# Two changes to the norms of a two-layer encoder: where the squares are summed, and who adds the old x

## The chip, the cores and the metric

The kernel runs on one core of a Trainium2 chip. A core has five engines that run side by side, each through its own list of instructions in order: TensorE (PE, matmuls), VectorE (DVE), ScalarE (ACT), GpSimd (POOL), and SyncE (SP), which here only issues DMAs. They meet by semaphores: an instruction that needs another engine's result waits, and everything behind it on its engine waits too. The metric is the device time of one execution in microseconds (us); lower is better. Before the change it is 2510.55 us, the median of 3 runs (2510.04 to 2511.96).

## The reference

Two layers are applied, with the same weights, to two groups of 512 and 256 tokens of 1024 channels. Cut to what matters here:

```
def _rmsnorm(x, gain):
    xf = xf * lax.rsqrt(jnp.mean(xf * xf, axis=-1, keepdims=True) + EPS)
    return xf * gain

for l in range(2):
    h = _rmsnorm(x, norm_mix_pre[l])          # the norm that begins a layer
    mix = ... projections, four attentions, gates, w_out of h ...
    x = x + _rmsnorm(mix, norm_mix_post[l])   # middle of a layer
    hf = _rmsnorm(x, norm_ffn_pre[l])
    f = _conv_ffn(hf, ...)
    x = x + _rmsnorm(f, norm_ffn_post[l])     # end of a layer
```

Between the two layers there are thus two norms in a row: `x + _rmsnorm(f, norm_ffn_post[0])`, and at once `_rmsnorm` of that sum with `norm_mix_pre[1]`, whose result h feeds the first matmuls of the second layer.

## The kernel before, in words

**Layout.** Activations lie transposed, with channels on the 128 partitions: x is 8 blocks of 128 channels by 768 tokens (512 + 256), kept in DRAM between norms. The tokens are cut into three groups of 256, G0, G1 and G2, so that the norms of one group can run while PE works on another. Every operand of a matmul is split into a high and a low part in float32r, and each product is three matmuls (high by high, high by low, low by high), L842 to L854.

**A norm.** `pre_norm` (L716) makes h for one group. ACT squares four tiles of 128x512 (two channel blocks by 256 tokens each). A sum over channels is a sum over partitions, which PE does by matmuls against a column of 1/1024: `mean_square` gives four small matmuls for one such tile (`b<-const,p`, 128x2; each is two passes in the trace, so x8). Then `rstd_bcast`: DVE adds epsilon (L499), POOL takes the power -0.5 (L505), PE transposes that value over all partitions (L464). Then DVE multiplies the four tiles, ACT copies the high part of h, and DVE subtracts to make the low part. The gain is multiplied in place beforehand, on ACT. With `easy` (the norm in the middle of a layer) the four squares are summed on DVE first and PE sums one tile; without it (the first norm of the kernel, and the norm between the layers) each tile has its own mean square on PE.

**Between the layers.** `grouped_tail` ends the down projection group by group. When a group is through, `sandwich` (L786) runs for it: loads the old x into four buffers `p` by DMA, takes the mean square of the group (already collected in `msq`), multiplies by 1/rms, adds the old x, stores the new x (`x<-g`), and calls `pre_norm` for the next layer. While it does, PE goes on with the tail of the next group, and after G2's tail with the first matmuls of the next layer, which take h of G0, then G1, then G2 (`v_tiles` and `job_V`: per group 96 matmuls of 256 columns).

**The order.** `Flow` is a planner that runs while the program is built: it keeps a clock per engine with a cost for each operation, and whoever is ready first gets its instructions written next. So a changed cost or dependence moves instructions on all engines near it. On the chip each engine then follows its list. There are 12 buffers `p`, 13 `g` (the residual tiles `g` of this norm among them), 4 PSUM buffers `b` and 2 `d`.

**Names.** `p` squares and loads, `g` the residual tiles, `b` and `d` PSUM, `st` the rstd values, `h` the normed input, `raw` and `w` a weight unit before and after its split, `x` in DRAM. L460 is every matmul, L464 every transpose, L476 every ACT operation, L490 every tensor_tensor on DVE, L509 every DMA.

Of the kernel before, what the change touches and what calls it, by code (L numbers as in the profile page):

```python
# [20 lines left out]
ALU = mybir.AluOpType  # L21
# [411 lines left out]
class Trunk:  # L433
# [74 lines left out]
    def dma(self, out, in_, *deps):  # L508
# [3 lines left out]
            nbytes *= s  # L512
        return self.f.on("dma", max(nbytes / 340.0, 450), *deps) + 2000


    def w_init(self):
        self.w_fetched = self.w_split = self.w_used = 0
        self.w_raw, self.w_ready = {}, {}
        self.w_allowed = 0
        self.spare = True  # L520
        self.parts = []
        self.tail_keys = {("out", m) for m in range(KB - TAIL_OUT, KB)}
        self.tail_keys |= {("down", len(CHUNKS) - 1, m) for m in range(KB - TAIL_DOWN, KB)}
        self.w_total = self.depth * len(self.keys)
        self.steps = unit_steps(self.keys, self.depth)
        self.paired = {n + i for s, n in self.steps if s == "first" for i in range(2)}
# [191 lines left out]
    def pre_norm(self, G, x, gain, h, last, first=False, easy=False):  # L718


        c = slice(GRP * G, GRP * G + GRP)
        b = yield from self.B.get([128, 512], F32)
        for i, (ap, t, free) in enumerate(x):
            q = yield from self.P.get([128, 2, GRP], F32)
            if first:
                yield t
            t = q.t = self.act(q.ap, ap, AF.Square, t, q.t)
            if not easy:
                yield t
                t = self.mean_square(b, q.ap, not i, i == len(x) - 1, t)  # L730
                q.drop(t)
            elif i:
                t = sq.t = self.tt(sq.ap, sq.ap, q.ap, ALU.add, t, sq.t)
                q.drop(t)
            else:
                sq = q
        if easy:
            yield t
            t = self.mean_square(b, sq.ap, True, True, t)
            sq.drop(t)  # L740
        yield t
        r = self.rstd_bcast(b, 2, t)
        tn = next(r)
        xg = []
        for i, (ap, t, free) in enumerate(x):
            for j in range(2):
                t = self.copy(ap[:, j], ap[:, j], free, scale=gain[:, 2 * i + j : 2 * i + j + 1])
            xg.append(t)
        if first:
            self.w_allowed = max(self.w_allowed, 1)  # L750
            self.pump()
        yield tn
        for w in r:
            yield w
        for i, (ap, _, _) in enumerate(x):
            if easy:
                yield from self.calm()
            xg[i] = t = self.tt(ap, ap, self.over(b, 2), ALU.mult, xg[i], b.t)
        b.drop(t)
        for i, (ap, _, _) in enumerate(x):  # L760
            k = slice(2 * i, 2 * i + 2)
            t = self.copy(h[:, 0, k, c], ap, xg[i], h.t)
            if easy:
                yield from self.calm()
            t = self.tt(h[:, 1, k, c], ap, h.f32()[:, 0, k, c], ALU.subtract, t)
        last(t)
        self.h_ready[G] = t
        self.w_allowed = len(self.steps)
# [14 lines left out]
    def sandwich(self, G, mix, msq, x_old, x_new, pre, h, done=None):  # L783

        c = slice(GRP * G, GRP * G + GRP)
        easy = done is not None
        xs = []
        for i in range(4):  # L790
            x = yield from self.P.get([128, 2, GRP], F32)
            x.t = self.dma(x.ap, x_old[:, 2 * i : 2 * i + 2, c], x.t)
            xs.append(x)
        b = yield from self.B.get([128, 512], F32)
        sq = msq[G]
        self.add_square(sq)
        yield sq.t
        t = self.mean_square(b, sq.ap, True, True, sq.t)
        sq.drop(t)
        yield t  # L800
        yield from self.rstd_bcast(b, 2, t)
        new = []
        for i, m in enumerate(mix):
            if easy:
                yield from self.calm()
            t = self.tt(m[:, :, c], m[:, :, c], self.over(b, 2), ALU.mult, b.t, m.t)
            if easy:
                yield from self.calm()
            t = self.tt(m[:, :, c], m[:, :, c], xs[i].ap, ALU.add, xs[i].t, t)
            xs[i].drop(t)  # L810
            new.append((m[:, :, c], t, self.dma(x_new[:, 2 * i : 2 * i + 2, c], m[:, :, c], t)))
        b.drop(t)
        if h is None:
            for m in mix:
                m.drop(t + 2500)
        else:
            yield from self.pre_norm(G, new, pre, h, done or (lambda t: [m.drop(t) for m in mix]),
                                     easy=easy)
# [33 lines left out]
    def grouped_tail(self, tail, nk, key, rhs, wait, mix, msq, gain, sandwich, acc=None):  # L852


        m0 = KB - tail
        for m in range(m0):
            yield from self.mix_buf(mix, m)
            w = yield from self.weight(key(m))
            blk = yield from self.dblock()
            blk.t = yield from self.mblock(self.whole(blk), w, rhs, nk, wait=None if m else wait)  # L860
            w.drop()
            yield from self.mix_evac(blk.cols, blk, m, range(3), mix, msq, gain, acc)
        ws = []
        for G in range(3):
            for m in range(m0, KB):
                yield from self.mix_buf(mix, m)
                if G == 0:
                    w = yield from self.weight(key(m))
                    ws.append(w)
                w = ws[m - m0]  # L870
                blk = yield from self.bank(G == 2)
                c0 = GRP * G
                src = blk[:, 0:GRP]
                blk.t = yield from self.mblock([(src, c0, c0 + GRP)], w, rhs, nk)
                if G == 2:
                    w.drop()
                yield from self.mix_evac(lambda c0, c1: src, blk, m, [G], mix, msq, gain, acc)
            self.f.start(sandwich(G), 0)
# [843 lines left out]
    def g_wait(self, gs, f):  # L1722
        while len(gs[f]) < 2:
            yield self.f.now + 200
        while max(t for _, t in gs[f]) > self.f.now:
            yield max(t for _, t in gs[f])

    def ffn(self, gain, sandwich, box):
        gs = [[] for _ in range(NF)]
        self.up_over, self.a_dram, self.v_dram, self.gelus = False, {}, {}, {}  # L1730
# [288 lines left out]
```

## Time and profile before

| | |
|---|---|
| median of 3 runs | 2510.55 us |
| the profiled execution | 2509.54 us |
| its span, first to last instruction | 2507.7 us |
| PE busy | 2462.9 us, 98% |
| DVE busy | 1714.1 us, 68% |
| ACT busy | 1284.6 us, 51% |
| POOL busy | 41.3 us, 2% |
| mean granted clock of PE | 0.993 |

The span is cut at three places by what PE does. From 0 to 70.2 us it starts up: weights and x arrive, the first norm runs, and the first matmuls of layer 0 follow. From 1225.9 to 1312.0 us lies the border of the two layers. From 2450 us the last norm runs out. Elsewhere PE has hardly a gap. DVE, ACT and the DMAs matter only where PE waits for them.

### The profile page before, as it was taken

The page shows a single profiled execution, that of the slowest core. Times are in us where ns is not written, and L with a number is a line of the kernel's source. Part 1 is how long each engine was busy: PE and PEld are TensorE (multiplying, and loading weights), DVE is VectorE, ACT ScalarE, POOL GpSimd, SP SyncE. Part 2 cuts the span into 40 slices and gives each one's busy share as a digit, 9 for nine tenths or more (in the row PEclk, how much of TensorE's full clock was granted, in tenths as well). Part 3 has the DMA queues.
Part 4 walks back from the last instruction along what each step waited for, and adds up shares of the span by engine and source line. Part 5 has one row for each costly group of instructions (what it writes and reads, how often), then busy time and mean ns, then how long its engine had stood idle before and what let it go on. Part 6 is the DMA issues. An engine that isn't in the chain of part 4 may idle for free. (4 is left out here: it accounts for less than half of the span.)

```text
span 2507.7 us, 40638 instructions
## 1 busy us (share of the span) xinstructions
PE 2462.9 (98%) x15606; PEld 2295.4 (92%) x15606; DVE 1714.1 (68%) x3282; ACT 1284.6 (51%) x2496; POOL 41.3 (2%) x38
## 2 busy tenths in 40 slices
PE   7999999999999999999989999999999999999998
PEld 7998888888999999988988988888889999999887
DVE  3567666756468888786755676667564689887866
ACT  5565665532355655563545556655324555556533
POOL 0001000000000000000000010000000000000000
PEclk9999999999999999999989999999999999999999
DMA  3433355343333333363423432553433233333643
GB/s 116 136 113 97 104 159 147 111 135 120 102 118 118 112 110 108 112 219 122 142 74 130 126 102 79 168 144 122 141 104 127 90 117 114 121 118 120 201 141 105
DMA packets 163986, 309.93 MB, mean 124 GB/s; under 512 B 25936, under 2 KB 89808, under 8 KB 163792
## 3 DMA queue, kind: packets, MB, share of 16 engines
q1 hardware_dynamic: 163792, 307.34, 39.0%
q8 instruction: 123, 2.02, 0.3%
q14 instruction: 71, 0.58, 0.1%
HBM read 225.74 MB, written 62.65 MB: 115 GB/s over the span
## 5 line engine op out<-in xcount | busy, mean ns | idle before, releaser
L460 PE MATMUL d<-h,w 128*128 128x256 f32 (+2 forms) x5040 | 920.0, 332 | 0.0
L460 PEld LDWEIGHTS d<-h,w 128*128 128x128 f32 x5040 | 762.2, 189 | 79.1
L460 PE MATMUL d<-g,w 128*128 128x256 f32 (+2 forms) x2763 | 489.7, 332 | 4.1 <-ACT g L476 3.6
L460 PEld LDWEIGHTS d<-g,w 128*128 128x128 f32 x2763 | 436.7, 188 | 39.7 <-ACT g L476 7.6
L490 DVE TENSOR_TENSOR w<-raw,w 128x1024 fp32r<-128x1024 f32 (+3 forms) x216 | 237.9, 1104 | 188.5 <-ACT w L476 184.4
L476 ACT ACTIVATE w<-raw 128x1024 fp32r<-128x1024 f32 (+3 forms) x216 | 206.5, 958 | 106.1 <-PE d L460 69.9
L476 ACT ACTIVATE p<-p,st 128x512 f32<-128x512 f32 (+2 forms) x288 | 174.4, 612 | 159.8 <-DVE st L1185 82.3
L460 PE MATMUL b<-h,w 128*128 128x384 f32 (+2 forms) x1344 | 233.5, 328 | 0.0
L460 PEld LDWEIGHTS b<-h,w 128*128 128x128 f32 x1344 | 213.4, 189 | 9.8
L460 PE MATMUL b<-g,w 128*128 128x384 f32 (+2 forms) x1257 | 215.2, 324 | 0.0
L476 ACT ACTIVATE g<-d 128x384 f32<-128x384 f32 (+6 forms) x210 | 113.1, 546 | 198.5 <-PE d L460 174.5
L460 PEld LDWEIGHTS b<-g,w 128*128 128x128 f32 x1257 | 203.2, 188 | 2.9
L494 DVE SCALAR_TENSOR_TENSOR p<-g,par,p 128x511 f32<-128x511 f32 (+1 forms) x232 | 142.3, 615 | 12.4 <-ACT p L476 8.2
L490 DVE TENSOR_TENSOR g<-g,b 128x512 f32<-128x512 f32 (+2 forms) x180 | 105.7, 598 | 62.3 <-PE b L460 43.7
L476 ACT ACTIVATE p<-b 128x512 fp32r<-128x512 f32 (+3 forms) x182 | 96.1, 538 | 93.0 <-PE b L464 73.3
L490 DVE TENSOR_TENSOR p<-b,p 128x512 fp32r<-128x512 f32 (+1 forms) x164 | 101.0, 627 | 50.5 <-ACT p L476 42.8
L490 DVE TENSOR_TENSOR g<-g,d 128x768 f32<-128x768 f32 (+2 forms) x118 | 80.0, 681 | 74.3 <-PE d L460 74.2
L460 PE MATMUL b<-g,g 128*128 128x384 f32 (+2 forms) x384 | 106.7, 348 | 5.1 <-DVE st L1158 3.3
L476 ACT ACTIVATE p<-g,par 128x512 f32<-128x512 f32 (+1 forms) x116 | 81.5, 703 | 54.6 <-DVE g L490 53.8
L476 ACT ACTIVATE g<-p 128x512 fp32r<-128x512 f32 (+1 forms) x118 | 67.5, 574 | 79.7 <-DVE p L490 58.2
L460 PE MATMUL b<-p,g 128*128 128x256 f32 x576 | 94.9, 286 | 3.1 <-DVE p L490 3.1
L1158 DVE CUSTOM_DVE_ANT_0 p<-b,bi 128x512 f32<-128x512 f32 (+2 forms) x144 | 81.5, 566 | 22.9 <-PE b L460 19.3
(120 smaller groups left out, 3156.6 us busy)
## 6 DMA issues: line engine op xcount, KB each, us to landing
raw<-weights SPq DMA_DIRECT2D x206, 512.0 KB, 3.9
bi<-weights SPq DMA_DIRECT2D x48, 512.0 KB, 3.8
g<-g SPq DMA_DIRECT2D x128, 96.0 KB, 2.2
p<-v SPq DMA_DIRECT2D x44, 256.0 KB, 3.7
x<-g SPq DMA_DIRECT2D x36, 256.0 KB, 2.1
p<-x SPq DMA_DIRECT2D x36, 256.0 KB, 4.5
v<-g SPq DMA_DIRECT2D x18, 384.0 KB, 3.8
v<-p SPq DMA_DIRECT2D x26, 256.0 KB, 2.0
```

The source lines that it names most:

```text
L460: self.nc.tensor.matmul(out=out, lhsT=lhsT, rhs=rhs, start=start, stop=stop, skip_group_check=more)
L476: self.nc.scalar.activation(out=out, in_=in_, func=func, **k)
L490: self.nc.vector.tensor_tensor(out=out, in0=a, in1=b, op=op)
L494: self.nc.vector.scalar_tensor_tensor(out=out, in0=a, scalar=s, in1=b, op0=op0, op1=op1)
L1158: nc.vector.tensor_tensor_reduce(out=p[:, :nkey], in0=s[:, :nkey], in1=bt, scale=1.0, scalar=init, op0=ALU.add, op1=ALU.max, accum_out=mx[ ...
```

## The change

The first part is in `pre_norm`: without `easy` the squares are now summed on DVE as well (three adds of 128x512 per group), and PE takes the mean square of one tile where it took four. That holds for the three groups of the first norm and the three between the layers. The second part is in `sandwich`, between the layers only: the four loads of the old x and the four adds on DVE go; instead, after each multiplication, a DMA issued by POOL adds the old x from DRAM onto the tile in place. The stores of the new x are issued after that, one by one.

```
+    def dma_add(self, out, in_, *deps):
+        self.nc.gpsimd.dma_start(out=out, in_=in_, accum_op=ALU.add)
+        nbytes = 4
+        for s in out.shape:
+            nbytes *= s
+        return self.f.on("dma", max(nbytes / 170.0, 450), *deps) + 2500
...
             t = q.t = self.act(q.ap, ap, AF.Square, t, q.t)
-            if not easy:
-                yield t
-                t = self.mean_square(b, q.ap, not i, i == len(x) - 1, t)
-                q.drop(t)
-            elif i:
+            if i:
+                if first:
+                    yield t
                 t = sq.t = self.tt(sq.ap, sq.ap, q.ap, ALU.add, t, sq.t)
                 q.drop(t)
             else:
                 sq = q
-        if easy:
-            yield t
-            t = self.mean_square(b, sq.ap, True, True, t)
-            sq.drop(t)
+        yield t
+        t = self.mean_square(b, sq.ap, True, True, t)
+        sq.drop(t)
...
+        by_dma = not easy and h is not None
-        for i in range(4):
+        for i in range(0 if by_dma else 4):
             x = yield from self.P.get([128, 2, GRP], F32)
             x.t = self.dma(x.ap, x_old[:, 2 * i : 2 * i + 2, c], x.t)
             xs.append(x)
...
             t = self.tt(m[:, :, c], m[:, :, c], self.over(b, 2), ALU.mult, b.t, m.t)
-            if easy:
-                yield from self.calm()
-            t = self.tt(m[:, :, c], m[:, :, c], xs[i].ap, ALU.add, xs[i].t, t)
-            xs[i].drop(t)
+            if by_dma:
+                t = self.dma_add(m[:, :, c], x_old[:, 2 * i : 2 * i + 2, c], t)
+            else:
+                if easy:
+                    yield from self.calm()
+                t = self.tt(m[:, :, c], m[:, :, c], xs[i].ap, ALU.add, xs[i].t, t)
+                xs[i].drop(t)
+            added.append(t)
+        b.drop(t)
+        for i, m in enumerate(mix):
+            t = added[i]
+            if by_dma:
+                yield t
             new.append((m[:, :, c], t, self.dma(x_new[:, 2 * i : 2 * i + 2, c], m[:, :, c], t)))
-        b.drop(t)
```

With the numbers of the buffers left out, the four lists of PE, DVE, ACT and SP differ only at the start and at the border of the layers; everything between, and the end, stands in the same order.

PE at the start of the program, before. `b_130`, `b_118` and `b_203` hold the mean squares of G0, G1 and G2, `st_155` is the rstd of G0, and `d_219<-w_166,h_93` are the first matmuls of the layer, on G0:

```order
L460 MATMUL b_130<-const,p_131 128x2 x4
L460 MATMUL b_130<-const,p_137 128x2 x4
L460 MATMUL b_130<-const,p_143 128x2 x4
L460 MATMUL b_130<-const,p_149 128x2 x4
L464 MATMUL b_130<-const,st_155 128x128 x2
L460 MATMUL b_118<-const,p_119 128x2 x4
L460 MATMUL b_118<-const,p_195 128x2 x4
L460 MATMUL b_203<-const,p_204 128x2 x4
L460 MATMUL d_219<-w_166,h_93 128x256 x6
L460 MATMUL b_118<-const,p_210 128x2 x4
```

PE there now (`b_130` and `b_118` as before, `w_157` and `w_179` the first two weight units):

```order
L460 MATMUL b_130<-const,p_131 128x2 x4
L464 MATMUL b_130<-const,st_146 128x128 x2
L460 MATMUL d_197<-w_157,h_93 128x256 x12
L460 MATMUL d_197<-w_179,h_93 128x256 x12
L460 MATMUL b_118<-const,p_119 128x2 x4
L460 MATMUL d_241<-w_157,h_93 128x256 x12
```

The three mean squares of G1 and G2 that stood ahead of the layer's first matmuls have gone, and the one that is left for G1 stands behind 24 of them.

PE at the border of the layers, now: `b_12870` is the mean square and rstd of G2 for the post norm, `b_12874` those of G1 and `b_13063` those of G2 for the next layer; `d_12961` and `d_13009` are projections of G0, `b_13049` and `b_13091` the values of G1:

```order
L460 MATMUL b_12870<-const,p_12278 128x2 x4
L460 MATMUL b_12874<-const,p_12875 128x2 x4
L460 MATMUL d_12961<-h_11747,w_12814 128x256 x23
L464 MATMUL b_12870<-const,st_12954 128x128 x2
L460 MATMUL d_12961<-h_11747,w_12814 128x256
L464 MATMUL b_12874<-const,st_12963 128x128 x2
L460 MATMUL d_13009<-h_11747,w_12841 128x256 x24
L460 MATMUL b_13049<-w_12286,h_11747 128x256 x12
L460 MATMUL b_13049<-w_12336,h_11747 128x256 x12
L460 MATMUL b_13091<-w_12286,h_11747 128x256 x12
L460 MATMUL b_13091<-w_12336,h_11747 128x256 x6
L460 MATMUL b_13063<-const,p_13064 128x2 x4
```

Before, G2's four mean squares (`b_13095`) stood ahead of G1's values, three of them together behind 12 matmuls:

```order
L464 MATMUL b_12780<-const,st_13036 128x128 x2
L460 MATMUL d_13066<-h_11774,w_12911 128x256 x12
L460 MATMUL b_13095<-const,p_13096 128x2 x4
L460 MATMUL b_13095<-const,p_13126 128x2 x4
L460 MATMUL b_13095<-const,p_13132 128x2 x4
L460 MATMUL b_13140<-w_12313,h_11774 128x256 x6
L460 MATMUL b_13095<-const,p_13138 128x2 x4
```

Between G2's transpose and its next mean square there are now 67 matmuls of 256 columns, where there were 13 before the first of four.

POOL at the border, now, word for word; `st_12520`, `st_12688` and `st_12954` are the rstd of G0, G1 and G2 in the post norm, `st_12733` and `st_12963` those of G0 and G1 for the next layer:

```order
L505 TENSOR_TENSOR st_12520<-st_12520,const 128x2
L517 DMA g_10903<-x_123 128x2x256
L517 DMA g_10954<-x_123 128x2x256
L517 DMA g_11010<-x_123 128x2x256
L517 DMA g_11061<-x_123 128x2x256
L505 TENSOR_TENSOR st_12688<-st_12688,const 128x2
L505 TENSOR_TENSOR st_12733<-st_12733,const 128x2
L517 DMA g_10903<-x_123 128x2x256
```

Twelve DMAs, three times four, have come between POOL's small operations, which stood alone there.

## Rows read from the trace of the kernel before

**Rows 1.** Busy time by stretch; then granted clock, DMA share, GB/s.
```profile
core 0: us, PE busy (x) PEld busy (x) DVE busy (x) ACT busy (x) POOL busy (x), PEclk, DMA share, GB/s
0.00:26.00 26.00, 12.74 (x58) 12.28 (x59) 8.34 (x12) 14.96 (x25) 1.84 (x5) 1.00 0.58 187
26.00:70.20 44.20, 44.20 (x333) 44.20 (x334) 16.84 (x34) 19.65 (x44) 1.40 (x2) 1.00 0.17 55
...
1225.90:1312.00 86.10, 78.97 (x607) 78.47 (x606) 47.78 (x96) 42.58 (x93) 4.15 (x6) 0.88 0.24 80
```

**Rows 2.** Timeline of PE, 0 to 80 us: start, length, instructions, idle before.
```profile
7.49 6.96 PE L460 MATMUL b<-const,p 128*128 128x2 f32 x32 [7.49 <-DMA const<-const]
...
20.91 5.28 PE L460 MATMUL b<-const,p 128*128 128x2 f32 x24 [3.81 <-ACT p L476]
26.05 1.63 PE L460 MATMUL d<-w,h 128*128 128x256 f32 x6
...
33.31 5.17 PE L460 MATMUL d<-w,h 128*128 128x256 f32 x30
...
52.94 5.92 PE L460 MATMUL d<-h,w 128*128 128x256 f32 x48
...
70.22 8.64 PE L460 MATMUL b<-h,bi 128*128 128x512 f32 x48
```

**Rows 3.** Timeline of PE, 1225 to 1320 us.
```profile
1252.10 0.95 PE L460 MATMUL b<-const,p 128*128 128x2 f32 x8
1252.91 1.32 PE L460 MATMUL b<-g,w 128*128 128x256 f32 x9
...
1256.95 1.05 PE L460 MATMUL b<-const,p 128*128 128x2 f32 x8 [0.92 <-ACT p L476]
1257.86 4.60 PE L460 MATMUL d<-w,h 128*128 128x256 f32 x24
1262.30 3.04 PE L460 MATMUL b<-w,h 128*128 128x256 f32 x24
...
1280.58 3.58 PE L460 MATMUL b<-const,p 128*128 128x2 f32 x16 [5.82 <-ACT p L476]
...
1312.01 8.17 PE L460 MATMUL b<-h,bi 128*128 128x512 f32 x45
```

**Rows 4.** Busy time by stretch (columns as in rows 1): the slow stretch.
```profile
1285.00:1290.00 5.00, 5.00 (x25) 5.00 (x25) 0.16 (x1) 0.00 (x0) 0.70 (x1) 0.50 0.00 0
```

**Rows 5.** DVE by line and shape, 1225 to 1312 us: busy us, mean ns.
```profile
L490 DVE TENSOR_TENSOR g<-g,b 128x512 f32<-128x512 f32 x24 | 15.6, 680 | 4.4 <-PE b L464 4.4
L490 DVE TENSOR_TENSOR g<-g,p 128x512 f32<-128x512 f32 x12 | 8.3, 692 | 0.4
```

**Rows 6.** Timeline of ACT, 0 to 27 us: squares, gains, first weight.
```profile
6.46 0.63 ACT L476 ACTIVATE p<-p 128x512 f32<-128x512 f32 x1 [1.68 <-DMA p<-x_in]
9.42 0.63 ACT L476 ACTIVATE p<-p 128x512 f32<-128x512 f32 x1 [2.32 <-PE b L460]
9.95 3.28 ACT L476 ACTIVATE p<-p,par 128x256 f32<-128x256 f32 x8
13.14 1.04 ACT L476 ACTIVATE w<-raw 128x1024 fp32r<-128x1024 f32 x1
```

**Rows 7.** Timeline of all engines, 0 to 45 us: the rstd of G0 and what follows.
```profile
14.57 1.23 DVE L490 TENSOR_TENSOR w<-raw,w 128x1024 fp32r<-128x1024 f32 x1
14.72 1.63 POOL L505 TENSOR_TENSOR st<-st,const 128x2 f32<-128x2 f32 x1 [14.28 <-DVE st L499]
...
17.14 2.48 DVE L490 TENSOR_TENSOR p<-p,b 128x512 f32<-128x512 f32 x4 [1.34 <-PE b L464]
```

**Rows 8.** POOL's operation L505, 1225 to 1312 us: ns, least, median, most.
```profile
L505 POOL TENSOR_TENSOR st<-st,const x6: 697/698/699, 1227.2 to 1287.5; 128x2 f32<-128x2 f32 x6
```

**Rows 9.** DMA issues, 1262 to 1272 us: KB each, median us to landing.
```profile
p<-x SPq DMA_DIRECT2D x4, 256.0 KB, 4.9
```

**Rows 10.** Timeline of all engines, 1225 to 1320 us: G0's first multiplication.
```profile
1228.55 0.69 DVE L490 TENSOR_TENSOR g<-g,b 128x512 f32<-128x512 f32 x1 [0.51 <-PE b L464]
```

More of the change, by code (lines that the diff above doesn't have):

```diff
@@ L801, in sandwich @@
         yield from self.rstd_bcast(b, 2, t)
-        new = []
+        new, added = [], []
         for i, m in enumerate(mix):
```

## The prediction

> **What bounds the kernel now.** I read the stretches first [rows 1]. PE is busy 44.20 of 44.20 us from 26.0 to 70.2, and it is so nearly everywhere else; it is short of work in the first 26 us (12.74 busy) and at the border of the layers, where 86.1 us hold 78.97 us of PE at a mean granted clock of 0.88. So the time is PE's work plus what PE loses at these two places and at the very end. The planner's lists change only at the first two, so the sum needs nothing else.
>
> Then the timelines. At the start [rows 2] the reader sees PE's first matmuls of the layer at 26.05, behind 24 small passes at 20.91 that waited for ACT. At the border [rows 3] PE waits 0.92 us at 1256.95 and 5.82 us at 1280.58, both for ACT's squares `p`. After each the matmuls are slow: 24 of 256 columns take 4.44 us from 1257.86 to 1262.30, against 0.120 us each in full run (144 from 52.94 to 70.22 [rows 2]), 2.88 us. From 1285 to 1290 the clock column reads 0.50, the lower of the two levels (1.2 GHz) [rows 4]. At the start the column reads 1.00 [rows 1], but at 33.31 PE still takes 5.17 us for 30 matmuls [rows 2], so there I go by the spacing.
>
> **The change part by part.**
>
> *Small matmuls.* Per group three mean squares of eight passes go. At full clock one costs PE 0.81 us (1252.10 to 1252.91 [rows 3]); nine at the border are 7.3 us, all on the path. The DVE adds that take their place (three of 128x512 per group, 0.69 us by the nearest add [rows 5]) are 2.1 us per group, but only the last one lies behind the last square, since ACT's squares come 0.6 us apart.
>
> *The start.* The first norm's chain was: third square at 6.46, fourth at 9.42, held 2.32 us by PE, because its buffer came free only when PE had read an earlier square [rows 6]. Now it comes free when DVE has added one: third square 6.46 to 7.09, add to 7.8, fourth square 7.9 to 8.5. ACT's gains (3.28 us) and first weight copy (1.04) then end at 12.85, against 14.18 [rows 6]; DVE's weight split (1.23 [rows 7]) ends at 14.1. The mean square is ready earlier: last add at 9.3, eight passes at the cold spacing of 6.96/32 = 0.22 us [rows 2] to 11.0, POOL and transpose to about 13. So the four multiplications start at 14.1, behind the split, where they stood at 17.14 [rows 7]: 3.0 us. Four take 2.48 us, and the first low part of h is ready 0.6 us later, at 17.2. PE's first matmul can then start at about 17.3, since the 24 small passes that stood ahead of it are gone from there (first fence of PE): 8.7 us before 26.05.
>
> From there PE has 288 matmuls of 256 columns to the row at 70.22. At 0.120 they are 34.6 us; two mean squares 2.3, six transposes 0.5, short waits for weights and h 0.6. The slow spacing lasted before from 20.91 to about 36 (of the 30 matmuls at 33.31, 13 at 0.23 and 17 at 0.12 give 5.0 us). The same 15 us from 17.3 cover 57 matmuls, 0.11 too long each: 6.3. Sum: 17.3 + 34.6 + 2.3 + 0.5 + 0.6 + 6.3 = 61.6, against 70.22: **8.6 us saved**. Between 3 + 3 (the multiplications' 3.0 and three small groups at 1 us, if weights keep PE at the old pace) and 9.5. The cover is the weights' arrival; raw units come sooner too, since each is fetched when a split frees its buffer.
>
> *The border, work alone.* From 1225.9 to 1312.0 PE has 473 matmuls of 256 columns (56.8 us), 12 transposes (1.5) and before 15 mean squares (12.2): 70.5 us; the other 15.6 are waits and slow clock. Now there are 6 mean squares, 4.9 us: 63.2. So the new stretch is 63.2 + S, and all turns on S.
>
> *The old x.* The twelve loads go and twelve adds of 692 ns on DVE [rows 5]. So G2's four multiplications (680 ns) run back to back, 2.5 us, where eight operations took 5.4, and G1's norm behind them on DVE comes 2.7 us earlier. In return nothing of x is there beforehand: the accumulating DMA starts after the multiplication, and squares, stores and gains of the next norm wait for it. Call D the time from the end of a group's last multiplication until its last add has landed. POOL is free (0.70 us per small operation [rows 8]); behind the adds stand only later rstd operations there. On ACT the squares wait, and behind them evacuations of the next tail; on SP the stores, and one weight load. The gains wait for the stores, as before, and lengthen nothing while rstd is still being made.
>
> No DMA of POOL and no accumulating one is in the trace. The lower bound for D is the load of the same bytes, 4.9 us to landing [rows 9]; below that I see no reason to go, since an add moves at least those bytes and can't start before its multiplication. The upper bound is four, one after the other without overlap: 19.6 us from the first, 17.7 after the last multiplication. I take **D = 8**, nearer the load, which is the same tensor, pattern and place: 4.9, 0.7 for POOL, and 2.4 for a second reading (of the destination).
>
> The Trainium skill ("DMA: Bandwidth & Descriptors", Anatomy of one DMA) gives POOL's DMAs 2.0 us plus bytes/436 GB/s, an estimate of 2.6 us for one add; by that D would lie under 5 and G2's wait below would vanish. No run here shows it.
>
> How much D is hidden is counted in the new order of PE (0.120 us a matmul, 0.81 a mean square). G0: transposes end and multiplications run from 1228.55 [rows 10] to 1231.0; 113 matmuls and one mean square stand before PE wants G0's new squares, at 1242.9. Less last square and add (1.3), D up to 10.5 costs nothing. G1: 108 matmuls, likewise up to 9.9. G2 has the 67 of the fence. After G2's transpose DVE needs 0.3 + 2.5 (G2) + 2.5 (G1) + 0.6 until G1's h has its first low part, 5.9, while PE has 25 matmuls, 3.2: a wait of 2.6, which the new order brings. Another 42 matmuls later, 10.8 after the transpose, PE wants G2's squares; less 1.3 and the 2.8 at which the multiplications ended, D is hidden up to 6.6. At D = 8 PE waits 1.4. G2's transpose itself I put 0.9 late, since DVE's epsilon stands behind two value splits and a weight split. Each of the two waits may drop the clock: 1.6 us each, as the 0.92 us wait did (4.44 - 2.88). S = 2.6 + 1.4 + 0.9 + 3.3 = 8.2. The border is 71.4 instead of 86.1: **14.7 saved**.
>
> *Sum.* 8.6 + 14.7 = 23.3 off the profiled 2509.54: 2486.2. The median of the runs stands 1.0 above that execution, so **2487.2 us**.
>
> **The rivals.**
>
> *The adds are quick* (D at or under 6.6): S loses 1.4 and 1.6, 2484. For it speaks that DMAs are idle around there, shares of 0.24 [rows 1]; against it that an add must wait for POOL and reads twice.
>
> *The start gives less.* PE goes early but waits for weights: 6.0 instead of 8.6, or 5.0, about 2490. Before, a weight's arrival never held PE at the start [rows 2], but PE was late itself.
>
> *DVE holds POOL up.* POOL's operation took 1.63 us at 14.72, beside a DVE operation with two inputs in SBUF that ended at 15.80 [rows 7], and 0.70 in all six at the border [rows 8]. If POOL's writing of descriptors is held in the same way, G2's adds go out only when DVE's train (eight multiplications, four subtractions, 7.4 us) is over, 4.9 later than the last multiplication; D is 11 to 12, G2's wait near 5 and the clock costs as after 5.82 us, twenty-four matmuls more at half speed: some 6 us more, 2493. Against it: the multiplications read PSUM and only one SBUF input. The Trainium skill ("SBUF — State Buffer", Who interferes with whom) says that a DVE instruction with two SBUF inputs contends with a GpSimd instruction that reads SBUF, and that what GpSimd needs for descriptors is taken only in DVE's two-port modes, which tensor_tensor lacks. By that rule this rival fails; the 1.63 agrees with its first half.
>
> *The adds run one after another* (slower side). At D = 17.7 G0 waits 7.2, G1 7.8, G2 11.1, one behind the other because each group's mean square stands in PE's list; with 2.6 + 0.9 and 5 us of slow clock after each (1280.58 to 1291) S is 44.6, the border 107.8, 21.7 more than before: 2510.5 + 21.7 - 8.6 = 2523.6. It decides from D = 14 on: there waits of 3.5 + 4.1 + 7.4 with 3.5 and 13 of clock make S 31.5, which is 22.9 + 8.6. For it: a destination that is read and written back may not stream as loads do, and all four go through one queue that is new here. Against it: four loads land in 4.9 together with a weight.
>
> **How the numbers follow.** The forecast has 0.45, quick adds 0.15, a lesser start 0.13, DVE holding POOL 0.12, serial adds 0.13 (of which 0.09 end slower, the rest between 2500 and 2515), and 0.02 is left for what I don't see. A measurement of this kernel tells about 0.2% (5 us) from no change. Faster by more 0.87, within 0.03, slower 0.10. The range is 2479 to 2506: below, all waits of S gone but G1's and a start of 9.5; above, D = 13.
>
> **What would show it.** Right: first matmul with `h` near 17 us, the row `b<-h,bi` near 62 instead of 70.2; from G0's mean square for the post norm to the next layer's `b<-h,bi` about 71 us; one wait of PE for DVE's h of G1, one of 1 to 2 us for DVE's sum of squares of G2; 4 to 8 us from a POOL DMA's issue to its landing. Wrong: PE or ACT waits of more than 5 us for these DMAs, G0's and G1's adds landing after PE wants them, or a start that still waits at 20 us for weights.

## The result and the profile after

The changed kernel takes **2491.15 us**, the median of 4 runs (2490.79 to 2493.42); the kernel before, run beside it, 2510.30 (4 runs, 2505.98 to 2511.96). The ratio is 0.9928, 95% interval [0.9911, 0.9945]. The profiled execution took 2491.35 us with a span of 2489.6, which is 18.1 less than before, at a mean granted clock of 0.995. So the change is faster by 0.7%. The time lies 3.95 us above the forecast of 2487.2 and inside its range.

The stretches first, cut where the changed kernel has the same rows (columns as in [rows 1]): to PE's first row of 23 matmuls, to the first `b<-h,bi`, a piece of the border, and the border from G0's mean square for the post norm to the next `b<-h,bi`.

```profile
0.00:16.59 16.59, 3.14 (x12) 2.37 (x12) 6.51 (x11) 10.86 (x20) 0.91 (x5) 1.00 0.80 263
16.59:60.90 44.31, 40.94 (x307) 39.87 (x308) 24.55 (x45) 23.58 (x51) 1.40 (x2) 0.96 0.22 66
...
1258.73:1277.60 18.87, 15.97 (x104) 15.40 (x105) 11.40 (x22) 9.55 (x21) 6.33 (x6) 0.82 0.66 141
...
1218.44:1295.75 77.31, 68.94 (x535) 67.64 (x534) 45.38 (x93) 42.79 (x93) 19.18 (x18) 0.93 0.49 103
```

The start is through at 60.90 where [rows 2] had 70.22: 9.3 us saved. The border takes 77.3 us instead of 86.1: 8.8 saved. These two make the 18.1; beside them layer 0 came out 1.8 us longer and layer 1 1.8 shorter, with the same lists, which cancels. PE's instructions at the border fall from 607 to 535, which is nine mean squares of eight passes each. What PE does not fill of the 77.3 is 8.4.

PE's timeline of the changed kernel at the start, which answers to [rows 2]; the bracket holds the idle time before and its releaser:

```profile
8.88 1.87 PE L460 MATMUL b<-const,p 128*128 128x2 f32 x8 [8.88 <-DVE p L490]
11.79 0.69 PE L464 MATMUL b<-const,st 128*128 128x128 f32 x2 [1.03 <-POOL st L505]
14.91 0.58 PE L460 MATMUL d<-w,h 128*128 128x256 f32 x1 [2.44 <-ACT h L476]
16.59 4.43 PE L460 MATMUL d<-w,h 128*128 128x256 f32 x23 [1.09 <-DVE h L490]
21.72 1.05 PE L460 MATMUL b<-const,p 128*128 128x2 f32 x8 [0.71 <-DVE p L490]
...
29.24 3.11 PE L460 MATMUL d<-h,w 128*128 128x256 f32 x24 [0.38 <-DVE g L490]
...
34.02 3.01 PE L460 MATMUL b<-w,h 128*128 128x256 f32 x23 [1.29 <-DVE h L490]
38.02 1.05 PE L460 MATMUL b<-const,p 128*128 128x2 f32 x8 [0.99 <-DVE p L490]
```

The other engines there, timeline of all of them, for [rows 6, 7]:

```profile
7.47 0.63 ACT L476 ACTIVATE p<-p 128x512 f32<-128x512 f32 x1 [0.18 <-DMA p<-x_in]
...
11.03 0.70 POOL L505 TENSOR_TENSOR st<-st,const 128x2 f32<-128x2 f32 x1 [10.58 <-DVE st L499]
...
12.32 1.22 DVE L490 TENSOR_TENSOR w<-raw,w 128x1024 fp32r<-128x1024 f32 x1 [1.37 <-ACT w L476]
13.46 2.47 DVE L490 TENSOR_TENSOR p<-p,b 128x512 f32<-128x512 f32 x4
```

The fourth square no longer waits for PE; the rstd is made before the weight split and not beside it; and the multiplications start at 13.46, right behind that split, instead of 17.14.

PE's timeline at the border, for [rows 3]. What to see are the brackets:

```profile
1218.44 0.95 PE L460 MATMUL b<-const,p 128*128 128x2 f32 x8
...
1245.68 3.10 PE L460 MATMUL d<-w,h 128*128 128x256 f32 x24 [1.56 <-DVE g L490]
1249.12 3.13 PE L460 MATMUL d<-w,h 128*128 128x256 f32 x24 [0.34 <-DVE g L490]
1253.08 1.31 PE L460 MATMUL b<-const,p 128*128 128x2 f32 x8 [0.83 <-DVE p L490]
1257.00 1.87 PE L460 MATMUL b<-const,p 128*128 128x2 f32 x8 [2.61 <-DVE p L490]
1258.73 4.46 PE L460 MATMUL d<-h,w 128*128 128x256 f32 x23
...
1267.24 0.38 PE L460 MATMUL b<-w,h 128*128 128x256 f32 x1 [0.61 <-ACT h L476]
1268.97 6.63 PE L460 MATMUL b<-w,h 128*128 128x256 f32 x41 [1.35 <-DVE h L490]
1276.54 1.02 PE L460 MATMUL b<-const,p 128*128 128x2 f32 x8 [0.93 <-DVE p L490]
...
1295.75 8.64 PE L460 MATMUL b<-h,bi 128*128 128x512 f32 x48
```

The wait of 5.82 has gone. In its place stand two that the forecast named, G1's h (0.61 and 1.35) and G2's squares (0.93), and four that it did not: 1.56, 0.34, 0.83 and 2.61.

For these, DVE's timeline of the same place:

```profile
1237.27 2.80 DVE L490 TENSOR_TENSOR g<-g,b 128x512 f32<-128x512 f32 x5
1239.99 0.41 DVE L490 TENSOR_TENSOR p<-p,s 128x256 f32<-128x256 f32 x1
1240.33 2.47 DVE L490 TENSOR_TENSOR g<-g,b 128x512 f32<-128x512 f32 x4
1242.72 2.49 DVE L490 TENSOR_TENSOR h<-g,h 128x512 fp32r<-128x512 f32 x4
1245.12 0.41 DVE L490 TENSOR_TENSOR g<-g,d 128x256 f32<-128x256 f32 x1
...
1247.51 1.23 DVE L490 TENSOR_TENSOR w<-raw,w 128x1024 fp32r<-128x1024 f32 x1 [1.64 <-ACT w L476]
1248.65 0.41 DVE L490 TENSOR_TENSOR g<-g,d 128x256 f32<-128x256 f32 x1
...
1251.04 1.23 DVE L490 TENSOR_TENSOR w<-raw,w 128x1024 fp32r<-128x1024 f32 x1 [1.64 <-ACT w L476]
1252.19 0.41 DVE L490 TENSOR_TENSOR g<-g,b 128x256 f32<-128x256 f32 x1
```

From 1237.27 to 1245.1 DVE is full, nearly all of it with the norms (G1's post norm, G0's next norm, G0's subtractions). Only then come the last three evacuations of G2's tail, `g<-g,d` twice and `g<-g,b`. The first two free the `d` buffers for which PE waits 1.56 and 0.34 us. ACT's squares that feed PE's next two mean squares stand behind them on ACT, and PE waits 0.83 and 2.61 for those. The evacuations stand 3.53 us apart, since DVE's list has a weight split between each two, and that waits for ACT's copy behind ACT's square and gain of the evacuation before.

POOL at the border, its timeline, and under it the landings of that stretch (KB each, median us from issue to landing):

```profile
1222.32 5.09 POOL L517 DMA_DIRECT2D g<-x  x4 [1.89 <-DVE g L490]
...
1264.65 4.93 POOL L517 DMA_DIRECT2D g<-x  x4 [2.61 <-issue]
```

```profile
q0 software_dynamic: 3264, 3.15, 25.6%
...
g<-x POOLq DMA_DIRECT2D x12, 256.0 KB, 6.3
x<-g SPq DMA_DIRECT2D x12, 256.0 KB, 4.4
```

An accumulating DMA holds POOL for 1.25 us and lands 6.3 us after its issue. D is read from the timelines of DVE and ACT:

```profile
1233.05 0.63 ACT L476 ACTIVATE p<-g 128x512 f32<-128x512 f32 x1 [0.73 <-DMA g<-x]
...
1263.45 4.87 DVE L490 TENSOR_TENSOR g<-g,b 128x512 f32<-128x512 f32 x8 [2.82 <-PE b L464]
...
1275.04 0.63 ACT L476 ACTIVATE p<-g 128x512 f32<-128x512 f32 x1 [1.46 <-DMA g<-x]
```

G0's last multiplication ended at about 1223.5 and ACT's fourth square started at 1233.05, after waiting for the DMA: D = 9.5. For G2 the first four of the eight multiplications end at about 1265.9, and the fourth square starts at 1275.04: 9.1.

### The profile page after: what moved, and what is told of

Its sections match the earlier page's. It is cut to its first block, busy times and chain, and to the rows that moved or that the text cites. A ratio compares the mean times of both kernels' runs of the same rounds, so it can differ in the third digit from the quotient of the medians.

```text
span 2489.6 us, 40390 instructions
## 1 busy us (share of the span) xinstructions
PE 2438.8 (98%) x15462; PEld 2268.6 (91%) x15462; DVE 1717.3 (69%) x3288; ACT 1284.6 (52%) x2496; POOL 55.3 (2%) x50
## 3 DMA queue, kind: packets, MB, share of 16 engines
q0 software_dynamic: 3264, 3.15, 0.9%
## 5 line engine op out<-in xcount | busy, mean ns | idle before, releaser
L460 PE MATMUL d<-g,w 128*128 128x512 f32 (+2 forms) x2778 | 491.7, 332 | 5.5 <-ACT g L476 5.0
```

The costliest lines, as they stand in the source:

```text
L460: self.nc.tensor.matmul(out=out, lhsT=lhsT, rhs=rhs, start=start, stop=stop, skip_group_check=more)
```

## The experiments

Two theories stood at the beginning. A: the summed squares bring all of the gain, at the start and at the border, and the accumulating DMA brings nothing, since DVE's adds were not what PE waited for. The rival: a part of the border's gain comes from the DMA, which takes twelve adds off DVE. Four kernels take the change apart. The edits are against the changed kernel; the first block gives them in words, the others are cut from the diffs.

**Only the first norm's squares summed** (border as before), and **only the border changed** (first norm as before).

```
 e1_start:   if not (first or easy): mean square of each tile   # as before at the border
             by_dma = False
 e2_border:  if first: mean square of each tile                 # as before at the start
```

> Only the first norm's squares are summed on the vector engine; the border of the layers is as before. Theory A (the two places gain by themselves and their gains add: 9.3 us at the start, 8.8 at the border by the two traces): the row b<-h,bi at 60.9 instead of 70.2 us, the border's stretch 86.1 us as before, time 9.3 below the kernel before, about 2501. Rival B (starting early only moves a later limit, the weights' arrival, so that the gain is given back in layer 0, which took 1.8 us longer in the changed kernel): 2503 to 2508, with layer 0 longer by what was won.

> Only the border is changed (squares summed and the old x added by the accumulating DMA); the first norm is as before. Theory A: start 70.2 us as before, border's stretch 77.3 instead of 86.1, time about 2501.5. Rival B (the start's gain is the only real one, the border's is eaten by waits that differ from run to run): 2506 to 2510.

Measured: 2499.81 us, ratio to before 0.9961 [0.9947, 0.9975], and 2499.47, 0.9960 [0.9947, 0.9973]; before beside them 2508.66. The first has its `b<-h,bi` at 59.34 and a border of 84.9 with the waits of before (0.92, 0.39, 5.82); the second starts as before (68.01) and has a border of 77.4 with the waits of the changed kernel (1.56, 0.34, 0.82, 2.61, 0.62, 1.35, 0.54). The gains, 8.9 and 9.2, add to 18.0, against 19.2 and, in a repeat below, 17.2 for both together: within the noise the halves do not touch each other.

**Sums without the accumulating DMA**, and **the accumulating DMA without the sums at the border.**

```
-        by_dma = not easy and h is not None
+        by_dma = False                                          # e3_sum_loads
...
+            if not (first or easy):                             # e4_dma_nosum
+                yield t
+                t = self.mean_square(b, q.ap, not i, i == len(x) - 1, t)
```

> Squares summed at both places, but the old x loaded beforehand and added on the vector engine as before, no accumulating DMA. Theory A (at the border the gain is PE's nine small groups, 7.3 us, and the accumulating DMA gives little: it spares 2.8 us of vector work per group and costs about 1 us of wait): border 77 to 80 us, time 2491 to 2494. Rival R1 (the accumulating DMA is what pays at the border): border 84 to 86, time 2499 to 2501. Rival R2 (the DMA costs more than the adds it spares, since its last add lands 9 us after the last multiplication): border 72 to 75, time 2486 to 2489.

> First norm summed; at the border the accumulating DMA, but four mean squares per group on the matmul engine as before. Theory A: PE has 7.3 us more at the border, 84 to 86 us, time about 2498 to 2500. Rival R1 (the DMA is what pays): border 77 to 79, time 2491 to 2493. Rival R2 (the DMA costs): border 88 or more, time above 2502.

Measured: 2490.48, 0.9927 [0.9914, 0.9940]; and 2504.04, 0.9980 [0.9972, 0.9988]. The sums alone give the whole gain, as theory A had it; the border of the first is 79.05, with 1.19, 2.14, 0.41, 3.04 and 1.90 of waits. The second kernel is a miss for A: without the sums the DMA takes 4.2 us back from the 2499.81 of the start alone, and its border is 91.05, longer than the 84 to 86 that A gave it. The intervals of these two just overlap, but the border is 6.1 us longer than the 84.9 of the start alone. There rival R2 came true (88 or more, above 2502). One cause shows in its timelines of POOL and PE:

```profile
1265.69 4.94 POOL L517 DMA_DIRECT2D g<-x  x4 [4.67 <-ACT g L476]
1268.64 2.73 POOL L505 TENSOR_TENSOR st<-st,const 128x2 f32<-128x2 f32 x1
```

```profile
1271.43 0.43 PE L464 MATMUL b<-const,st 128*128 128x128 f32 x2 [2.14 <-POOL st L505]
```

The rstd, 0.70 us elsewhere, shows 2.73 beside and behind the four issues, and PE waits 2.14 for it. Here POOL's issuing holds PE directly. The other long waits are for h of G0 (2.52 and 1.35) and of G1 (1.38 and 1.34).

**Where the missing 6 us of the border went.** Theory C: the four unforeseen waits come from evacuations queued behind DVE's norms, and a planner that holds the norms back gets them back. Rival D (a theory, not the time D): the norms' work on DVE has to be done before h is there anyway, so that holding it back only makes h of G0 and G1 later. Theory E: the planner's wrong prices for the DMA place the work badly.

```
-            if easy:                     # in pre_norm, twice
+            if not first:                # e5_calm, e8_loads_calm, e9_calm_cost
                 yield from self.calm()
...
-            if easy:                     # in sandwich, before the multiplication
+            if h is not None:            # e5_calm, e8_loads_calm, e9_calm_cost
                 yield from self.calm()
...
-        return self.f.on("dma", max(nbytes / 170.0, 450), *deps) + 2500
+        return self.f.on("pool", 1250, *deps) + 5000     # e6_cost, e9_calm_cost
...
+        by_dma = False                   # e8_loads_calm
```

> The changed kernel, but between the layers the planner holds back each vector operation of the norms while the vector engine is more than 500 ns ahead (as it does in the middle of a layer), so that the tail's evacuations of PSUM come between them. Theory C (what the border still loses are waits behind trains of 8 to 12 vector operations of the norms: 1.56 and 0.34 us for PSUM buffers, 0.83 and 2.61 for squares queued behind late evacuations, 5.3 in all and slow clock after them): these waits go, border 71 to 74 us instead of 77.3, time 2485 to 2488. Rival D (the vector work has to be done before h is there anyway; held back, h of G0 and G1 comes later): border 77 or more, time 2490 to 2495.

> The changed kernel, with the planner told what the trace of it shows for an accumulating DMA (1.25 us on POOL each, 5 us more to landing, instead of 1.5 and 2.5): it puts G2's mean square for the next layer behind all of G1's matmuls. Theory C: the landing costs PE 0.9 us now and no more is to be had: 2489 to 2492. Rival E (the planner's wrong price for the landing is what the border loses): border 71 to 74, time 2484 to 2488.

> As the run with calm, but the old x loaded beforehand and added on the vector engine. Theory C: like the run with calm within 2 us, if the accumulating DMA gives nothing by itself; up to 4 us slower if the four adds per group, 2.8 us of vector work, matter once the trains are broken up. Rival D: 2490 to 2496.

> Calm and the corrected price of the accumulating DMA together. Theory C: as with calm alone or 1 us faster, 2484 to 2488. Rival E: the lower end, as fast as the run with the price alone. Rival D: 2490 to 2495.

Measured, with 2511.92 before: 2507.13 (0.9985 [0.9977, 0.9994]), 2497.85 (0.9952 [0.9939, 0.9964]), 2502.60 (0.9967 [0.9955, 0.9979]) and 2501.52 (0.9963 [0.9949, 0.9978]); borders of 92.6, 84.9, 92.3 and 88.4. All four are slower than the changed kernel; for the second the intervals just overlap (0.9928 [0.9911, 0.9945] for the changed kernel), but its border is 7 us longer. PE's timeline of the first of them:

```profile
1248.39 2.01 PE L460 MATMUL b<-const,p 128*128 128x2 f32 x8 [5.17 <-DVE p L490]
...
1267.67 1.87 PE L460 MATMUL b<-const,p 128*128 128x2 f32 x8 [5.00 <-DVE p L490]
```

C as a remedy is wrong, and E too: a planner with the right prices makes a worse list (it then waits 3.71 and 1.35 for G0's h). Rival D is right in sign and too small in size, and most of what PE waits for is not h but squares (5.17, 5.00 and 3.33, against 1.59 and 1.70 for G1's h and 2.15 for two rstd). The same holding back with loads instead of DMAs has as long a border (92.3), so the accumulating DMA is not what lengthens it. That kernel is 4.5 us faster (2502.60), but elsewhere, and what makes the difference isn't shown.

**Four last runs**: the changed kernel again; the DMA writing the old x over the tile; G2 by loads and only G0 and G1 by DMA; only the subtractions held back.

```
-        self.nc.gpsimd.dma_start(out=out, in_=in_, accum_op=ALU.add)
+        self.nc.gpsimd.dma_start(out=out, in_=in_)               # e12_plain
...
-        by_dma = not easy and h is not None
+        by_dma = not easy and h is not None and G < 2            # e10_mixed
...
-            if easy:                     # before the subtractions of pre_norm
+            if not first:                                        # e11_calm_sub
                 yield from self.calm()
```

> The changed kernel once more, beside the kernels it is compared with. Expected 2488.5 to 2493.5 us and the same waits of PE at the border (1.56, 0.83, 2.61, 0.61 + 1.35, 0.93 us): if its border or its start moves by over 1 us, differences of that size between kernels say nothing.

> The changed kernel with the twelve DMAs of POOL writing the old x over the tile instead of adding it: the same lists on every engine, and the sum with the old x is left out between the layers. Theory P (the length of D comes from POOL's issuing, 1.25 us each, and the flight of one DMA, not from the reading of the destination): issue to landing 6.0 to 6.5 us as before, D of G2 9.1, time 2489 to 2493. Rival Q (the second reading costs what the prediction gave it, 2.4 us): landing about 4 us, D of G2 about 6.7, the wait of 0.93 us for G2's squares gone, 2487 to 2490.

> The changed kernel, but G2, whose old x is the one that is wanted soonest, has its old x loaded beforehand and added on DVE (four adds of 0.69 us between its multiplications), while G0 and G1 keep the accumulating DMA. If D is only a matter of G2: the wait of 0.93 us goes and G2's h comes some 6 us earlier, but G1's h comes 2.8 us later on DVE, so the gain is 1 us at most: 2489 to 2493. Rival (D of G2 is what holds the border back beyond the row that shows it, through ACT's squares and gains): all of the later waits go, 2484 to 2487.

> The changed kernel, but the planner holds back the four subtractions of a group's low part at the border while DVE has work, so that the evacuations of the tail come before G0's subtractions; the multiplications that start the accumulating DMAs stay where they are. The lists then have both mean squares (G2's post norm, G1's) ahead of the first matmuls of the next layer, and G2's own after 65 of them. Theory A' (the waits of 1.56, 0.34, 0.83 and 2.61 us come from evacuations behind DVE's trains, and can be had back): they shrink to some 3 us, 2487 to 2490. Rival D' (what is moved up exposes the accumulating DMA of G2 instead: its squares are wanted about 8 us after its multiplications, less than D of 9.1 and the squares' 2.6): a wait of 3 to 6 us at G2's mean square, 2491 to 2496.

Measured, with 2508.20 before: 2491.03 (0.9936 [0.9921, 0.9952]), 2489.55 (0.9929 [0.9912, 0.9945]), 2496.47 (0.9953 [0.9938, 0.9968]), 2493.33 (0.9941 [0.9926, 0.9957]).

The repeat has the same waits to 0.1 us (1.56, 0.33, 0.82, 2.61, 0.62, 1.35, 1.03), a start of 60.82 and a border of 77.7. Its profiled span is 3.1 us longer than the first one's, of which the border holds 0.4: single spans differ by that much elsewhere.

The plain DMA is the telling one, since its lists are the changed kernel's on every engine. Its POOL timeline, landings, PE timeline and, from ACT's, G2's fourth square:

```profile
1263.67 2.90 POOL L517 DMA_DIRECT2D g<-x  x4 [3.21 <-issue]
```

```profile
q0 software_dynamic: 960, 3.15, 12.0%
...
g<-x POOLq DMA_DIRECT2D x12, 256.0 KB, 4.3
```

```profile
1251.51 1.31 PE L460 MATMUL b<-const,p 128*128 128x2 f32 x8 [0.82 <-DVE p L490]
1255.43 1.45 PE L460 MATMUL b<-const,p 128*128 128x2 f32 x8 [2.61 <-DVE p L490]
...
1267.99 5.18 PE L460 MATMUL b<-w,h 128*128 128x256 f32 x41 [1.35 <-DVE h L490]
1273.01 0.95 PE L460 MATMUL b<-const,p 128*128 128x2 f32 x8
```

```profile
1270.42 0.63 ACT L476 ACTIVATE p<-g 128x512 f32<-128x512 f32 x1 [0.23 <-DMA g<-x]
```

Without the adding the same bytes take 960 packets instead of 3264, POOL issues one in 0.73 us instead of 1.25, and it lands in 4.3 instead of 6.3: D of G2 is 5.5 (1264.9 to 1270.42) instead of 9.1. G2's wait has gone and with it some slow clock; the border is 75.2, 2.1 shorter. Rival Q holds for the landing, and the price is larger than it said: adding makes 3.6 of D. The times don't tell P from Q, since 2489.55 lies in both ranges. But the four unforeseen waits are there to 0.02 us. **They do not depend on how long these DMAs take**: that is shown. The order that the planner made with them is another matter: the kernel with loads has other waits.

Held-back subtractions gain nothing. PE's timeline of that kernel:

```profile
1246.97 1.92 PE L460 MATMUL b<-const,p 128*128 128x2 f32 x8 [6.55 <-DVE p L490]
1250.89 1.87 PE L460 MATMUL b<-const,p 128*128 128x2 f32 x8 [2.00 <-DVE p L490]
...
1266.85 1.05 PE L460 MATMUL b<-const,p 128*128 128x2 f32 x8 [2.08 <-DVE p L490]
```

The evacuations do come earlier, by 2.4 us counted from G0's mean square (7.05 us from the first to the last, as in the changed kernel); but G0's h is now behind them, both mean squares stand ahead of the layer's matmuls, and the border is 81.6. D' is right in that G2's mean square waits, 2.08 us, less than it said. With G2 by loads, PE reaches G2's mean square before DVE's eight operations are through:

```profile
1274.85 1.87 PE L460 MATMUL b<-const,p 128*128 128x2 f32 x8 [4.47 <-DVE p L490]
```

The border is 81.8, and the four early waits are there as before (1.57, 0.33, 0.82, 2.61). Neither theory had this: the planner put that mean square ahead of G1's values, and the wait moved with it. No kernel here that computes the whole sum beats the changed one by more than the intervals.

## Why the prediction was right, and where it was not

**The start** (8.6 forecast, 9.3 measured) went by its steps. The fourth square came at 7.47 (7.9 forecast), the multiplications at 13.46 (14.1). The second is early because ACT's gains and weight copy, which the split waits for, ended at 12.28 and not 12.85. POOL's operation took 0.70 and not the 1.63 of [rows 7], now that no split stands beside it, but the multiplications did not wait for it. That the sum came out is in part luck, for four of its terms were mis-sized and nearly cancel. The first matmul went at 14.91 and not 17.3, since it needs only the high part of h. The "short waits" are 4.5 (1.09, 0.71, 0.38, 1.29, 0.99) and not 0.6. Two mean squares at 0.81 are 1.6 and not 2.3, and slow clock and the rest cost about 4.8 and not 6.3. The lesser start fell: PE waited for no weight there. Over the twelve kernels with this start the row `b<-h,bi` lies between 58.7 and 61.1, and in two with the old one at 70.22 and 68.01, so one trace tells the saving to about 2 us.

**The border's work** was right: nine mean squares fewer, 63.2 of work left. **S was the failed step**: 8.2 forecast, 14.1 measured (77.3 - 63.2). The working counted the new order of PE at 0.120 us a matmul and let PE wait only for what hangs on the old x and on G2. It asked of every matmul whether its h was there, and never whether its PSUM buffer was free: 1.9 us. It noted evacuations of the next tail on ACT, but not that the squares of G2's post norm and of G1 stand behind late ones, and gave them no price: 3.4 us. The profiled execution missed its sum by 5.15 us (2491.35 against 2486.2): the border came out 5.9 longer, the start 0.7 shorter. The terms of S are:

| term of S | forecast | measured |
|---|---|---|
| `d` buffers and squares behind late evacuations | 0 | 1.56 + 0.34 + 0.83 + 2.61 = 5.3 |
| G1's h | 2.6 | 2.0 |
| G2's squares | 1.4 | 0.9 |
| G2's transpose late | 0.9 | 0 (slow matmuls kept PE from it until 1263.03) |
| slow clock | 3.3 | about 4.3 |
| what is left (the last matmul ahead of a wait is some 0.2 longer) | 0 | 1.6 |

The clock is read from rows: 23 matmuls take 4.30 from 1258.73 to the transposes where 2.76 is their full pace, 41 from 1268.97 take 6.63 against the 5.18 of the kernel with plain DMAs, and the mean squares at 1253.08 and 1257.00 lose 1.3; the stretch from 1258.73 has a granted clock of 0.82.

**D** was 9.1 to 9.5 against 8. That adding comes on top of the load's time was right: 2.0 us more to landing than a plain DMA. That it is a second reading of the destination is not shown. The other term was mis-sized: POOL's issuing was put at 0.7 and is 1.25, four in a row. The Trainium skill ("DMA: Bandwidth & Descriptors", Anatomy of one DMA) gives an estimate of 2.6 us for one such DMA by its fit; the traces show 4.3 for a plain and 6.3 for an adding one.

**The rivals.** Quick adds need D at or under 6.6: no; the plain DMA, at 5.5, shows that the mechanism itself was right and worth 2.1 us of border, where the rival had 3.0. Serial adds fell: four lie in 9.1, not 17.7. DVE holding POOL fell: G2's four issues took 4.93 beside DVE's train of multiplications, G0's 5.09 with gaps on DVE. The Trainium skill ("SBUF — State Buffer", Who interferes with whom) tells of a probe in which a `tensor_tensor` on DVE did not stall DMAs, and the trace agrees.

**What stays open** is what the last three evacuations would cost without the weight splits between them. That the four waits come from these evacuations, and that the splits set their spacing of 3.53 us, is read from the rows; no run took the waits away, and taking the splits out wasn't tried.

## What to carry to other kernels

When an order is counted out by hand, ask of every matmul two things, whether its input is there and whether its output buffer is free; the second stands in another engine's list. Here it cost 1.9 us, and inputs queued behind such evacuations 3.4 more. An accumulating DMA is not a free add: here it took twelve adds off DVE and gave nothing over loads and adds, and without the summed squares it cost 4.2 us. A planner with better prices, or with one kind of work held back, made no list better here: a tuned order is a balance, so test it whole.

## What the runs showed of the hardware

Twelve DMAs of 256 KB from POOL: adding, 1.25 us of POOL and 6.3 us to landing each, in 272 packets; plain, 0.73 us, 4.3 us and 80 packets. Stores of the new x land in 4.4 us (4.2 beside plain DMAs), where all stores of x in the kernel with loads have a median of 2.1. In one kernel (sums left out) a small operation of POOL behind such issues shows 2.73 us instead of 0.70.
